# RWKV/HGRN2 decoder layer: the output projection's activations are loaded before the last column of a block and split behind it

## The chip, the cores and the metric

The kernel runs on one core of a Trainium2 chip. A core has five engines that run their own instruction lists in order and wait for each other by semaphores: TensorE (PE, with PEld for its weight loads), VectorE (DVE), ScalarE (ACT), GpSimd (POOL) and SyncE (SP). SP and POOL mainly issue transfers (DMAs) between the chip's memory (HBM) and the core's; PE's results go to PSUM banks. The metric is the device time of one execution in microseconds (us), the median of three runs.

## The reference

One decoder layer, 2048 tokens, model width 1024. Two kinds of head groups work beside each other on one input projection, their outputs go through one output projection, and a feed-forward part with a causal convolution follows.

```python
h = rmsnorm(x)
proj = h @ w_in                                    # 1024 -> 2048 (HGRN2) + 1792 (RWKV-7)
o_hg = hgrn2_mixer(*split(proj[:, :2048], 4))      # 4 heads of 128, chunked linear recurrence
o_rw = rwkv7_mixer(*split(token_shift(proj[:, 2048:])))   # 8 heads of 64: r, k, v, decay, a, gate
x = x + concat([o_hg, o_rw]) @ w_out               # the output projection, 1024 -> 1024
x = x + conv_ffn(rmsnorm(x), w_up, w_down)         # 1024 -> 2 x 2816 -> 1024
return rmsnorm(x)
```

All is float32. A product is made of three matmuls on parts of its factors: each factor is split into a high part (a cast, on ACT) and a low part (the rest, a subtraction on DVE), and high x high, high x low and low x high are summed.

## The kernel before

The program has two phases. Phase 1 (to about 1300 us) goes over the 2048 tokens in four blocks of 512. `dense()` issues its work as a list of jobs: for each block 30 columns ("P") of the input projection, each 128 wide, as eight k by three matmuls into one PSUM bank "pj"; and out blocks ("O"), the output projection of a block. Beside it, two other streams issue RWKV's work (per block two "supers" of 256 channels) and HGRN2's (per head of a block). A driver takes pieces of the streams in turn, and after that a scheduler in the framework sets each engine's order from the recorded program, so that instructions of the three streams stand mixed. Buffers come from pools by tag, each tag with a number of tiles; a tile that is still read makes the next writer wait.

The out block of block 0 (called Out 1 here, about 529 to 636 us) is issued after the last column of block 1, that of block 1 (Out 2, 883 to 971 us) after the last column of block 2, and that of block 2 (Out 3, 1209 to 1298 us) after the last column of block 3. Block 3's output projection belongs to phase 2 and is left as it is.

`out_block` (L379) works in four quarters: `i2` is the half of the tokens, `dh` the half of the 512-wide output columns. In each quarter two token tiles of 128 get one pj bank each, and for each of eight k the weights `woraw` are loaded by POOL (tag wraw, four tiles, L395), split into `wh` (ACT, L254) and `wl` (DVE, L255) in tag w (four tiles), and used by two times three matmuls with `hh` and `hl`. At the end the input `xh` is added to the banks (DVE, L413) and sent to `x1d`. I call three such matmuls a triple.

The activations come from `oT`, to which the mixers write. In Out 1 and Out 2 each k of the first quarter loads a row of 128 x 512 (`oraw`, SP, L388, tag sg, two tiles) and splits it into `hh` (ACT, L247) and `hl` (DVE, L248). Out 3 has the first half of its tokens ready in `ohl`, loaded and split during the last columns; at its third quarter it loads the second half in eight pieces of 128 x 256 (L392). In the quarter with such loads, `xh` takes two of the four wraw tiles; in the others it takes tag sg.

`load(i)` (L570) gets a column's weights, two tiles of tag w for high and low parts. From the second block on they come from HBM copies `Win`, with four DMAs on POOL. When a column starts, `load(i + 1)` gets those of the next one. For the last column of a block this is the first column of the block after the out block (`Win280`, `Win281`), so that its weights lie in two of the four w tiles while the out block runs.

Steps of the mixers that stand around the out blocks and are named later: `Ti` is built by DVE row by row (L811, L813), then transposed to `TZ` (L817) and `TTs` (L823); PE's small products with `M` and `RHS` follow, and then eight steps of the recurrence, `XH` (PE L915, L920, DVE L922). `KBT` and `E` of the next super are made by DMAs on SP from `KBb` (L766) and `Ed` (L757). `UV` is an ACT copy out of PSUM. In HGRN2, `SH` is the state, `part` and `osq` belong to the norm of its output, `hX`, `hk` and `hq` to its chunks. Tags s0, s1 and s2 hold RWKV's r, k, v of a super, tag tl its decay inputs.

## Time and profile before

| | |
|---|---|
| runs | 2632.3, 2635.08, 2636.21 us (median 2635.08) |
| profiled execution | 2639.41 us |
| its span | 2637.6 us |
| PE busy | 2545.3 us (97% of the span) |
| DVE busy | 1968.2 us (75%) |
| ACT busy | 1384.5 us (52%) |
| POOL busy | 381.7 us (14%) |

The profile is of one execution on the chip. A window gives busy times of each engine between two points of the span; "PEclk" is the clock that PE was granted, as a share of full speed. A timeline row gives the start, the duration, the engine, the line, the operation, what it writes and reads, how many instructions are merged in the row, and in brackets how long the engine had stood idle before it and which instruction ended that. A helper's line (L247, L248, L254, L255, L270 to L272) is shared by all that call it, so that the names of the tiles tell what is meant.

### The profile page before, as it was taken

Reading aid. Unit: us, or ns where it says so; the run is one execution under the profiler, and the core shown is the slowest. Engines: PE = TensorE matmul, PEld = TensorE weight load, DVE = VectorE, ACT = ScalarE, POOL = GpSimd, SP = SyncE. Lnnn points to the kernel's source line nnn. Section 1 sums busy time; section 2 is a strip of 40 time slices with the busy share of each in tenths; the row PEclk is TensorE's granted clock in tenths of the full one; section 3 lists DMA queues with packets and bytes.
Section 4 is the critical chain, followed back from the end, with each engine's and each line's share of the span. In section 5 each row is a group of like instructions: output and inputs, shape, how many; then the busy total and the mean of one; then the engine's idle time right before and its main releaser. Section 6 shows DMA issues by size and latency. Waiting matters only on the chain.

```text
span 2637.6 us, 51053 instructions
## 1 busy us (share of the span) xinstructions
PE 2545.3 (97%) x19467; PEld 2046.8 (78%) x19467; DVE 1968.2 (75%) x3744; ACT 1384.5 (52%) x2266; POOL 381.7 (14%) x686
## 2 busy tenths in 40 slices
PE   7999999989999899999899999999999999999998
PEld 6877777767777677777688888887888888888887
DVE  5878676775576765787678799987998887766556
ACT  5566454555446554355466754556554554545444
POOL 6433222212222122222100000000000000000000
PEclk9999999989999999999899999999999999999999
DMA  8846463545655566755574477746764554998655
GB/s 309 236 161 191 159 167 119 148 145 200 195 170 141 168 204 181 252 181 161 193 251 136 130 233 260 235 158 217 243 204 132 170 171 131 333 321 284 200 190 188
DMA packets 380298, 518.98 MB, mean 197 GB/s; under 512 B 114463, under 2 KB 211093, under 8 KB 380053
## 3 DMA queue, kind: packets, MB, share of 16 engines
q1 hardware_dynamic: 325521, 337.38, 40.3%
q0 software_dynamic: 54464, 178.32, 20.9%
q8 instruction: 153, 2.51, 0.4%
q14 instruction: 92, 0.75, 0.1%
q10 hardware_dynamic: 68, 0.02, 0.0%
HBM read 372.99 MB, written 134.22 MB: 192 GB/s over the span
## 4 chain that ended last, share of the span: by engine, by line
PE 53%; issue 7%; DVE 6%; DMA 5%; ACT 4%; POOL 1%; SPq 0%; DVEq 0%; POOLq 0%; ACTq 0%
PE ua L270 5%; PE ua L272 5%; PE ua L271 5%; PE pj L270 3%; PE da L271 3%; PE da L270 3%; PE da L272 3%; PE ud L271 3%; PE pj L271 3%; PE ud L270 3%; PE ud L272 3%; PE pj L272 3%; PE db L271 2%; PE db L272 2%; PE db L270 2%
## 5 line engine op out<-in xcount | busy, mean ns | idle before, releaser
L270 PE MATMUL pj<-hh,wh 128*128 128x512 f32 x960 | 394.6, 411 | 8.2 <-issue 3.4
L272 PE MATMUL pj<-hh,wl 128*128 128x512 f32 x960 | 378.3, 394 | 0.0
L271 PE MATMUL pj<-hl,wh 128*128 128x512 f32 x960 | 377.7, 394 | 0.0
L270 PE MATMUL ua<-Bh,uwh 128*128 128x512 f32 x704 | 276.6, 393 | 2.3 <-ACT m L122 1.2
L272 PE MATMUL ua<-Bh,uwl 128*128 128x512 f32 x704 | 274.9, 391 | 0.0
L271 PE MATMUL ua<-Bl,uwh 128*128 128x512 f32 x704 | 274.5, 390 | 0.0
L270 PEld LDWEIGHTS pj<-hh,wh 128*128 128x128 f32 x960 | 181.2, 189 | 56.6 <-issue 10.1
L272 PEld LDWEIGHTS pj<-hh,wl 128*128 128x128 f32 x960 | 180.8, 188 | 41.0 <-issue 2.0
L271 PEld LDWEIGHTS pj<-hl,wh 128*128 128x128 f32 x960 | 181.5, 189 | 34.6 <-issue 1.6
L254 ACT CAST uwh<-uraw 128x512 fp32r<-128x512 f32 x220 | 134.5, 617 | 131.2 <-PE ua L271 54.7
L255 DVE TENSOR_TENSOR dal<-draw,dah 128x512 fp32r<-128x512 f32 x138 | 95.3, 691 | 108.3 <-ACT dah L254 106.9
L255 DVE TENSOR_TENSOR uwl<-uraw,uwh 128x512 fp32r<-128x512 f32 x220 | 147.4, 686 | 34.1 <-ACT uwh L254 33.8
L254 ACT CAST dah<-draw 128x512 fp32r<-128x512 f32 x138 | 85.7, 621 | 160.8 <-PE da L271 75.9
L270 PEld LDWEIGHTS ua<-Bh,uwh 128*128 128x128 f32 x704 | 132.4, 188 | 32.0 <-ACT m L122 3.8
L272 PEld LDWEIGHTS ua<-Bh,uwl 128*128 128x128 f32 x704 | 132.4, 188 | 27.9 <-DVE uwl L255 0.4
L271 PEld LDWEIGHTS ua<-Bl,uwh 128*128 128x128 f32 x704 | 132.3, 188 | 26.9
L1506 POOL DMA_DIRECT2D gd<-y x2 | 1.1, 542 | 948.8 <-DVE y L1504 948.8
L270 PE MATMUL ud<-Bh,uwh 128*128 128x512 f32 x352 | 138.2, 393 | 0.0
L272 PE MATMUL ud<-Bh,uwl 128*128 128x512 f32 x352 | 137.3, 390 | 0.0
L271 PE MATMUL ud<-Bl,uwh 128*128 128x512 f32 x352 | 137.2, 390 | 0.0
L271 PE MATMUL da<-dbl,dah 128*128 128x512 f32 x332 | 129.6, 390 | 0.3 <-DVE dbl L255 0.3
L272 PE MATMUL da<-dbh,dal 128*128 128x512 f32 x332 | 129.4, 390 | 0.0
(582 smaller groups left out, 6226.7 us busy)
## 6 DMA issues: line engine op xcount, KB each, us to landing
uraw<-in_w_up_dram SPq DMA_DIRECT2D x176, 256.0 KB
woraw<-in_w_out_dram POOLq DMA_DIRECT2D x96, 256.0 KB, 3.5
br<-gd SPq DMA_DIRECT2D x88, 256.0 KB
draw<-Sg SPq DMA_DIRECT2D x88, 256.0 KB
draw<-Tw SPq DMA_DIRECT2D x88, 256.0 KB
gd<-y SPq DMA_DIRECT2D x86, 256.0 KB
Sg<-br SPq DMA_DIRECT2D x72, 256.0 KB
xt<-x1d SPq DMA_DIRECT2D x32, 512.0 KB
```

The lines of the kernel that those rows point to most:

```text
L254: S.copy(hi, src)
L255: V.tensor_sub(lo, src, hi.bitcast(F32))
L270: TE.matmul(acc, lh, rh, start=first, stop=False, skip_group_check=skip)
L271: TE.matmul(acc, lh, rl, start=False, stop=False, skip_group_check=skip)
L272: TE.matmul(acc, ll, rh, start=False, stop=last, skip_group_check=skip)
L1506: (dma if end is None else nc.gpsimd.dma_start)(gd_[2 * h + b][fb * P:(fb + 1) * P, :], ys[0][:, b * BLK:(b + 1) * BLK])
```

## The change

A job "L" is put before the last column of blocks 1, 2 and 3, which waits until the mixers have written the outputs of the block concerned. For Out 1 and Out 2 it runs `o_load`: three loads of two rows each into the tiles of tags s0, s1 and s2 (`opair`) and two loads of one row into tags tl and sg (`oraw`). Behind the last column's matmuls of each k, `next_out` splits the rows whose places in `hh` and `hl` that column has read. For Out 3 it runs `o_half`: two loads of four half rows (`ohalf`) into s0 and s1, which are split in the second quarter instead of the third. `xh` always takes tag sg. The next column's weights are not loaded when a last column starts; for Out 1 and Out 2 `ahead` loads them at k = 3 of the last quarter's second half, for Out 3, after which no column comes, there is nothing to load.

```diff
--- before.py
+++ after.py
@@ -376,28 +376,20 @@
                 ready[k] += 1
             return f
 
-        def out_block(nb, oh=None, ol=None, then=None):
+        def out_block(nb, oh=None, ol=None, then=None, ahead=None):
 
 
             for i2 in range(2):
                 for dh in range(2):
                     accs = [bank("pj") for _ in range(2)]
                     for k in range(KD):
-                        if i2 == 0 and dh == 0 and oh is None:
-                            raw = stg("sg", "oraw", 2)
-                            dma(raw, oT[nb][k * P:(k + 1) * P, :])
-                            split_to(hh[:, k, :], hl[:, k, :], raw)
-                        if i2 == 1 and dh == 0 and oh is not None:
-                            raw = stg("sg", "oraw", 2)[:, 0:256]
-                            dma(raw, oT[nb][k * P:(k + 1) * P, 256:512])
-                            split_to(hh[:, k, 256:512], hl[:, k, 256:512], raw)
+                        if i2 == 0 and dh == 1 and oh is not None:
+                            split_to(hh[:, k, 256:512], hl[:, k, 256:512], rows["O2"][k // 4][:, k % 4, :])
                         raw = wp.tile([P, 512], F32, tag="wraw", name="woraw", bufs=4)
                         wload(raw, w_out[0, k * P:(k + 1) * P, dh * 512:dh * 512 + 512])
                         wh, wl = split(wp, raw, [P, 512], "w", 4)
                         if k == KD - 2:
-                            inputs = dh == 0 and (i2 == 0) == (oh is None)
-                            xh = [wp.tile([P, BLK], F32, tag="wraw", name="xh", bufs=4) if inputs else
-                                  stg("sg", "xh", 2) for _ in range(2)]
+                            xh = [stg("sg", "xh", 2) for _ in range(2)]
                             for q in range(2):
                                 t0 = nb * BLK + (i2 * 2 + q) * P
                                 dma(xh[q], x[0, t0:t0 + P, dh * 512:dh * 512 + 512])
@@ -408,6 +400,8 @@
                             mm3(accs[q], lhs, (wh, wl), k == 0, k == KD - 1)
                             if i2 == 1 and dh == 1 and q == 1:
                                 next_block(then, k)
+                                if k == 3 and ahead is not None:
+                                    ahead()
                             yield 680
                     for q in range(2):
                         V.tensor_add(xh[q], accs[q], xh[q])
@@ -463,11 +457,41 @@
             act(h4, src, AF.Copy, scale=w)
             V.scalar_tensor_tensor(l4, src, w, h4.bitcast(F32), ALU.mult, ALU.subtract)
 
+        def behind(k):
+
+            return [k - 2] if 2 <= k < KD - 1 else [k - 2, k - 1, k] if k == KD - 1 else []
+
         def next_block(nb, k):
 
             if nb is not None and nb < NBLK:
-                for k_ in ([k - 2] if 2 <= k < KD - 1 else [k - 2, k - 1, k] if k == KD - 1 else []):
+                for k_ in behind(k):
                     split_h(nb, k_)
+
+        def o_load(nb):
+
+            pieces = []
+            for u in range(3):
+                t_ = sp.tile([P, 2, BLK], F32, tag=f"s{u}", name="opair")
+                dma(t_, oT[nb][2 * u * P:2 * (u + 1) * P, :].rearrange("(k p) t -> p k t", p=P))
+                pieces += [t_[:, 0], t_[:, 1]]
+            for tag, bufs in (("tl", 1), ("sg", 2)):
+                pieces.append(stg(tag, "oraw", bufs))
+                k = len(pieces)
+                dma(pieces[-1], oT[nb][(k - 1) * P:k * P, :])
+            rows[("P", nb)] = pieces
+
+        def o_half(nb):
+
+            rows["O2"] = []
+            for u in range(2):
+                t_ = sp.tile([P, 4, 256], F32, tag=f"s{u}", name="ohalf")
+                dma(t_, oT[nb][4 * u * P:4 * (u + 1) * P, 256:512].rearrange("(k p) t -> p k t", p=P))
+                rows["O2"].append(t_)
+
+        def next_out(nb, k):
+
+            for k_ in behind(k):
+                split_to(hh[:, k_, :], hl[:, k_, :], rows[("P", nb)][k_])
 
         def sum_load(m):
 
@@ -559,6 +583,8 @@
             for m in range(2):
                 extra += [(at[3] + 14 + 5 * m, ("E", sum_load(m))), (at[3] + 17 + 5 * m, ("E", sum_make(m)))]
             extra += [(at[3] + 25 + m, ("W", 2, o_take(m))) for m in range(4)]
+            extra += [(len(jobs) - 1, ("L", 2))]
+            extra += [(at[nb] - 2, ("L", nb - 2)) for nb in range(2, NBLK)]
             for i, jb in sorted(extra, key=lambda e: e[0], reverse=True):
                 jobs.insert(i, jb)
             cols = [jb[1] for jb in jobs if jb[0] == "P"]
@@ -605,9 +631,15 @@
                     if jb[0] == "W":
                         jb[2]()
                     else:
-                        yield from (out_block(2, *rows["O"]) if jb[1] == 2 else out_block(jb[1], then=jb[1] + 2))
+                        yield from (out_block(2, *rows["O"]) if jb[1] == 2 else out_block(jb[1], then=jb[1] + 2, ahead=lambda i=i: load(i)))
+                    continue
+                if jb[0] == "L":
+                    while done["rw1"] < 2 * jb[1] + 4 or done["rw2"] < 2 * jb[1] + 2 or done["hg"] < 4 * jb[1] + 4:
+                        yield None
+                    (o_half if jb[1] == 2 else o_load)(jb[1])
                     continue
                 _, col, ev, cond, fin = jb
+                after = jobs[n + 1][1] if jobs[n + 1][0] == "O" and jobs[n + 1][1] < 2 else None
                 while not cond():
                     yield None
                 load(i)
@@ -616,7 +648,8 @@
                     next(ahead)
                     next(ahead)
                     constants()
-                load(i + 1)
+                if jobs[n + 1][0] != "O":
+                    load(i + 1)
                 i += 1
                 acc = bank("pj")
                 then = jobs[n + 1][1] if jobs[n + 1][0] == "A" else None
@@ -632,6 +665,8 @@
                         if fin is not None:
                             fin()
                     next_block(then, k)
+                    if after is not None:
+                        next_out(after, k)
                     yield 648 + 436 * aside
 
         def last_dma(nb):
```

The order moves on all engines around the three out blocks and stays as it was elsewhere; each engine has as many instructions as before, but for the loads. Lines in the new program are 35 higher from `rw_super` on.

ACT in Out 1, from the part around HGRN2's norm on (`Sf`, `osq`, `VT`) with `UV` and `RHS` of RWKV. Before:

```order
L122 ACTIVATE Sf<-hf 128x256
L122 ACTIVATE osq<-hg,eps_71 128x512
L122 ACTIVATE osq<-osq 128x512
L122 ACTIVATE VT<-hg 128x512
L122 ACTIVATE UV<-rw 64x8x128 x2
L247 CAST hh<-oraw 128x512 x2
L122 ACTIVATE RHS<-rw 128x8x64
L122 ACTIVATE RHS<-rw 64x8x64 x2
L254 CAST wh<-woraw 128x512
L247 CAST hh<-oraw 128x512 x2
L254 CAST wh<-woraw 128x512 x3
L247 CAST hh<-oraw 128x512 x2
```

With the change, from the place where `KT` and `Af` are done:

```order
L254 CAST wh<-woraw 128x512
L247 CAST hh<-oraw 128x512
L254 CAST wh<-woraw 128x512
L122 ACTIVATE osq<-hg 128x512
L247 CAST part<-osq 128x512
L122 ACTIVATE Sf<-hf 128x256
L122 ACTIVATE sgm<-pj 128x512
L122 ACTIVATE UV<-rw 64x8x128 x2
L247 CAST hh<-opair 128x512 x2
L247 CAST hh<-oraw 128x512
L118 ACT_TABLE_LOAD
L122 ACTIVATE osq<-hg,eps_71 128x512
```

Five casts hh stand earlier, four of them ahead of the rows shown; `UV` stands behind `part`, `Sf` and `sgm`, and three casts hh behind it.

SP at the same place, which issues the transfers of RWKV's next super and then the out block's. Before:

```order
L949 DMA oT_144<-yo 128x2x512
L766 DMA KBT<-KBb 32x16x32 x3
L754 DMA Ed<-M 32x16x32 x4
L766 DMA KBT<-KBb 32x16x32 x2
L757 DMA E<-Ed 64x1024 x2
L766 DMA KBT<-KBb 32x16x32 x11
L388 DMA oraw<-oT_143 128x512 x2
```

With the change:

```order
L984 DMA oT_144<-yo 128x2x512
L480 DMA oraw<-oT_143 128x512
L475 DMA opair<-oT_143 128x2x512 x2
L801 DMA KBT<-KBb 32x16x32 x3
L789 DMA Ed<-M 32x16x32 x4
L801 DMA KBT<-KBb 32x16x32 x2
L792 DMA E<-Ed 64x1024 x2
L801 DMA KBT<-KBb 32x16x32 x11
L475 DMA opair<-oT_143 128x2x512
L480 DMA oraw<-oT_143 128x512
```

Three of the five loads moved ahead of the first `KBT` transfers of the super, two stand behind the last of them.

PE in Out 3, at the end of the second quarter, after the last triple with `ohl`. Before:

```order
L915 MATMUL rw<-XH,M 64x64 x4
L920 MATMUL rw<-AR,XH 64x64 x4
L1000 MATMUL hg<-hX 32x16 x13
L915 MATMUL rw<-XH,M 64x64 x4
L920 MATMUL rw<-AR,XH 64x64 x4
L1000 MATMUL hg<-hX 32x16 x3
L915 MATMUL rw<-XH,M 64x64 x4
L920 MATMUL rw<-AR,XH 64x64 x4
L1000 MATMUL hg<-hX 32x16 x16
L915 MATMUL rw<-XH,M 64x64 x4
L920 MATMUL rw<-AR,XH 64x64 x4
L1007 MATMUL hg<-hX 32x32 x8
```

With the change:

```order
L950 MATMUL rw<-XH,M 64x64 x4
L955 MATMUL rw<-AR,XH 64x64 x4
L270 MATMUL pj<-wh,hh 128x512
L271 MATMUL pj<-wl,hh 128x512
L272 MATMUL pj<-wh,hl 128x512
L270 MATMUL pj<-wh,hh 128x512
L271 MATMUL pj<-wl,hh 128x512
L272 MATMUL pj<-wh,hl 128x512
L270 MATMUL pj<-wh,hh 128x512
L271 MATMUL pj<-wl,hh 128x512
L272 MATMUL pj<-wh,hl 128x512
L950 MATMUL rw<-XH,M 64x64 x4
```

The steps of the recurrence (`XH`) stood next to each other or with small HGRN2 products between them; now three triples with `hh` and `hl` follow the step shown, and the next two as well.

## The prediction

> **What bounds the kernel now.** I read the page's first part, then cut the stretches around the three out blocks into windows, then looked at PE's idle times one by one, and last at what each releaser had itself been waiting for.

> ```profile
> span 2637.6 us, 51053 instructions
> PE 2545.3 (97%) x19467; PEld 2046.8 (78%) x19467; DVE 1968.2 (75%) x3744; ACT 1384.5 (52%) x2266; POOL 381.7 (14%) x686
> ```

> PE is busy for 97% of the span, so no other engine's saving counts unless it takes an idle moment of PE away or a stretch in which PE runs at a lower clock. The change touches only the out blocks and their surroundings. In the windows the columns are start:end and length, busy time (and instructions) of PE, PEld, DVE, ACT and POOL, then granted PE clock, DMA share, GB/s.

> ```profile
> 540.00:546.30 6.30, 1.82 (x11) 0.86 (x12) 5.91 (x22) 5.10 (x8) 0.00 (x0) 0.82 0.15 59
> 546.30:551.00 4.70, 4.70 (x131) 4.17 (x132) 4.70 (x17) 2.62 (x5) 0.00 (x0) 0.52 0.38 117
> 536.00:564.00 28.00, 19.03 (x292) 14.67 (x290) 25.23 (x82) 17.41 (x28) 2.54 (x5) 0.88 0.40 127
> 564.00:580.00 16.00, 14.84 (x183) 10.19 (x184) 12.10 (x26) 5.96 (x13) 3.14 (x7) 0.68 0.53 177
> 580.00:636.00 56.00, 54.32 (x644) 40.36 (x644) 34.63 (x67) 31.14 (x53) 10.96 (x21) 1.00 0.41 133
> 883.00:919.00 36.00, 29.95 (x413) 20.82 (x413) 28.27 (x68) 22.41 (x41) 5.59 (x10) 1.00 0.53 169
> 919.00:971.00 52.00, 49.93 (x639) 36.99 (x639) 39.91 (x82) 29.48 (x48) 10.30 (x20) 1.00 0.47 150
> 1248.00:1263.00 15.00, 8.84 (x335) 7.10 (x331) 9.87 (x30) 1.64 (x3) 0.67 (x2) 0.93 0.53 168
> 1263.00:1268.00 5.00, 4.94 (x12) 3.72 (x12) 3.50 (x7) 2.69 (x9) 0.00 (x0) 0.54 0.56 189
> ```

> This is where time can come from. Out 1 (block 0's out block): PE idle is 28.00 - 19.03 = 8.97 us and 1.16 us in its first part, 1.68 us later. At reduced clock it also loses 0.48 x 4.7 = 2.3 us behind 546.3 and 0.32 x 16 = 5.1 us behind 564. Out 2 (block 1's): 6.05 and 2.07 us idle, no clock lost. Out 3 (block 2's): 6.16 us idle in 1248 to 1263, then 0.46 x 5 = 2.3 us of clock. That is 26.1 us idle and 9.7 us of clock, so 36 us is a ceiling.

> Next, who ends the idle times: the number in brackets is the idle time ahead of the instruction and its releaser.

> ```profile
> 538.71 0.49 PE L1075 MATMUL hg<-hq,SH 128*128 128x128 f32 x2 [1.01 <-DVE SH L1067]
> 541.45 0.50 PE L1094 MATMUL hg<-part,ones 128*128 128x512 f32 x1 [1.34 <-ACT part L247]
> 546.26 0.54 PE L1000 MATMUL hg<-hq,hk 128*32 128x32 f32 x22 [2.14 <-DVE hk L957]
> 558.92 0.50 PE L270 MATMUL pj<-wh,hh 128*128 128x512 f32 x1 [1.52 <-ACT hh L247]
> 563.89 0.50 PE L270 MATMUL pj<-wh,hh 128*128 128x512 f32 x1 [1.96 <-ACT hh L247]
> 885.82 0.49 PE L1075 MATMUL hg<-hq,SH 128*128 128x128 f32 x2 [1.72 <-DVE SH L1067]
> 1259.48 0.39 PE L915 MATMUL rw<-XH,M 64*64 64x64 f32 x6 [1.03 <-DVE XH L922]
> 1263.06 0.79 PE L270 MATMUL pj<-wh,hh 128*128 128x512 f32 x1 [3.01 <-ACT hh L247]
> 1262.60 0.40 ACT L247 CAST hh<-oraw 128x256 fp32r<-128x256 f32 x1 [8.04 <-DMA oraw<-oT]
> PE pj L270: 8.6, 6
> DMA oraw<-oT: 10.9, 5
> ```

> The last two rows are of the view of tile oraw: PE waited 8.6 us in six goes for it or for what is split from it, and its engines stood 10.9 us for its DMA. So the load is the late thing: at 1262.60 the cast had waited 8.04 us for its DMA and PE 3.01 us for the cast. The other idle times of Out 1 are no matter of oraw: they end with SH, part and hk, on DVE, which in 536 to 564 is itself busy for 25.23 of 28 us. There DVE, not PE, is the bound; whatever still has to pass through it has to be paid.

> **The change part by part.** It does not drop any arithmetic. Splits, weight casts and matmuls of the out block are as many as before.

> Loads ahead, Out 1 and Out 2. Eight oraw loads become three loads of a pair (opair) and two single ones, issued before the last column.

> ```profile
> 520.50 8.63 SPq L766 DMA_DIRECT2D KBT<-KBb  x11
> 529.23 9.33 SPq L388 DMA_DIRECT2D oraw<-oT  x2
> L247 ACT CAST hh<-oraw x24: 393/613/623, 546.7 to 1277.6; 128x512 fp32r<-128x512 f32 x16, 128x256 fp32r<-128x256 f32 x8
> L248 DVE TENSOR_TENSOR hl<-oraw,hh x24: 418/684/693, 548.1 to 1278.0; 128x512 fp32r<-128x512 f32 x16, 128x256 fp32r<-128x256 f32 x8
> ```

> Before, SP issues them from 529.2, behind the eleven KBT transfers. Three of the five new loads stand ahead of all KBT transfers of that super, the other two where the old ones stood, so five of the eight rows of o are there before the out block needs them. The splits are 8 x 0.61 = 4.9 us on ACT and 8 x 0.68 = 5.5 us on DVE as before. They only stand earlier, among the Ti adds of RWKV. What goes in Out 1 are the two waits for hh, 1.52 + 1.96 = 3.5 us, and the idle time that the out block's triples, now ready, can fill.

> What comes in its place is in the new order: all eight k of the first quarter stand ahead of TZ, and TZ, TTs and the evictions xh close it.

> ```profile
> 544.65 2.05 ACT L122 ACTIVATE UV<-rw 64x1024 f32<-64x1024 f32 x2
> 564.48 1.06 DVE L817 STREAM_TRANSPOSE TZ<-Ti 128x512 f32<-128x512 f32 x1
> 566.14 2.89 DVE L823 STREAM_TRANSPOSE TTs<-TZ 32x512 f32<-32x512 f32 x4
> 535.94 0.62 ACT L254 CAST wh<-woraw 128x512 fp32r<-128x512 f32 x1 [1.66 <-PE pj L271]
> 561.27 0.69 DVE L255 TENSOR_TENSOR wl<-woraw,wh 128x512 fp32r<-128x512 f32 x1 [0.25 <-ACT wh L254]
> ```

> First, ACT's UV pair now stands behind part, Sf and sgm, and PE's UV,M products are early in the quarter: I price this wait at the pair and a cast's length on each side, 2.05 + 0.62 + 0.39 = 3.1 us. Second, the weights of k = 4 and 5 are split behind Ti adds: two casts and two subtractions, 2 x (0.62 + 0.69) = 2.6 us. Third, TZ and TTs take 1.06 + 2.89 = 3.95 us on DVE at the quarter's end, of which the remaining triples hide about half: 2.0 us. Behind the waiting TTs on DVE stand the two xh adds, which free the pj banks for the next quarter, and behind the waiting UV on ACT the last three hh casts. Together 7.7 us of new waits.

> Of the idle 10.1 us, the waits for SH, part and hk (1.01 + 1.34 + 2.14 = 4.5 us) are DVE's, and triples between them hide half, so 2.2 stay. Of the 7.4 us of clock I leave half, 3.7, since new waits near 2 us stay. Out 1's gain: 10.1 + 7.4 - 2.2 - 3.7 - 7.7 = 3.9 us. The ends: nothing comes off SH, part and hk and no clock returns, 10.1 - 4.5 - 7.7 = -2.1; or all the clock returns and half the new waits are hidden, 17.5 - 4.5 - 3.9 = 9.1.

> On the clock: the rows show 0.52 behind a stretch where PE was busy for 1.82 of 6.3 us with no gap over 2.14 us, and 0.68 behind a gap of 1.96. [...]

> Out 2 has the same edit. Its idle 6.05 us holds 1.72 us for SH and, in three goes, 2.1 us for hh (engine, line, waited for: total, times, longest):

> ```profile
> PE pj L270 <- ACT hh L247: 2.1, 3, 0.9
> ```

> Half of SH stays (0.9), the third wait (2.0) comes whole and the second with 2.0, as the weights here meet single Ti adds; UV stands where it stood, though RHS behind it now follows five hh casts. The gain is 6.05 - 0.9 - 2.0 - 2.0 = 1.2 us. The ends: only the hh waits go and 3.1 + 2.0 come, 2.1 - 5.1 = -3.0; or the waits for hh and SH go and nothing comes, 3.8.

> Out 3. Two loads of four rows (ohalf), ahead of the KBT transfers, replace eight loads at the third quarter. PE's order had five XH steps in a row without an out triple between them and then the wait of 3.01 us; now three triples follow each step, some 9 matmuls:

> ```profile
> 566.58 0.63 PE L271 MATMUL pj<-wl,hh 128*128 128x512 f32 x1
> 551.28 0.40 PE L271 MATMUL pj<-wl,hh 128*128 128x512 f32 x1
> ```

> The 0.63 is one at low clock, 0.40 one at full. So 6.16 us idle (the 3.01 and 3.15 between the steps) and 2.3 us of clock can go, 8.5 us. Given back: eight hl subtractions of half width now stand ahead of TZ on DVE, 8 x 0.418 = 3.3 us, and I let all of it through to PE since the M chain behind TTs is what PE needs. Gain 8.5 - 3.3 = 5.2 us. The ends: 3.0 - 3.3, about 0; 8.5.

> Four weight tiles, xh in sg. The next column's weights held two of the four w tiles for the whole out block.

> ```profile
> ACT wh L254 <- PE pj L272: 25.5, 16, 3.4
> 636.01 0.50 PE L270 MATMUL pj<-hh,wh 128*128 128x512 f32 x1 [0.61 <-DVE xh L413]
> 971.24 0.50 PE L270 MATMUL pj<-hh,wh 128*128 128x512 f32 x1 [0.64 <-DVE xh L413]
> ```

> ACT waits 25.5 us for a free tile, yet PE's idle time in 580 to 636 and 919 to 971 is 1.68 + 2.07 us, and 1.25 of it is the xh wait around the next column. I take 0.5 us, ends 0 and 2.5.

> Late weights of the next column. They are now loaded behind the out block's last woraw on POOL:

> ```profile
> 624.04 0.54 POOL L395 DMA_DIRECT2D woraw<-in_w_out_dram  x1 [3.07 <-DVE wl L255]
> 963.20 0.54 POOL L395 DMA_DIRECT2D woraw<-in_w_out_dram  x1 [5.04 <-DVE wl L255]
> wh<-Win280h POOLq DMA_DIRECT2D x3, 256.0 KB, 5.3
> ```

> With 5.3 us to land, the first is there at 624.6 + 5.3 = 629.9 of the 636.0 where the column starts; in Out 2 at 963.7 + 5.3 = 969.0 of 971.2, and the last of the four three issues (1.6 us) later, 970.6. Cover is 4 us and under 1. I take 0; without cover it is at most the landing, 5.3 each.

> Sum: 3.9 + 1.2 + 5.2 + 0.5 + 0 = 10.8 us. The profiled execution took 2639.41 us (span 2637.6), 4.3 above the median of the runs; it becomes 2628.6, and the median of 2635.08 becomes **2624** us.

> **The rivals.** A, no change, 28%: DVE is the bound around Out 1 and Out 2 (25.23 of 28), so idle time only moves from hh to wl, UV and TTs; or the last two of the five loads still land late. For it: the splits are no fewer. Against it: in 580 to 636 DVE has 21 us free. With Out 1 and 2 at the mean of 3.9 and -2.1 and of 1.2 and -3.0, that is 0 together, and Out 3 at half, 2.6 us: 2632.

> B, slower, 12%: the new gaps bring the low clock to Out 2. Place: the UV or TTs wait of the first quarter. Gaps of 1.96 and 2.14 us stood ahead of a low clock, 1.72 did not, so it decides from about 2 us, and I expect 2.0 and more there. Price: another 5.1 us as in 564 to 580. Out 1 -2.1, Out 2 -3.0 - 5.1, Out 3 +2.6: -7.6 us, 2643. Against it: Out 2 had full clock with 6 us idle.

> C, all comes back, 8%: all three at their upper ends and 1 us of tiles, 9.1 + 3.8 + 8.5 + 1.0 = 22.4 us: 2613. For it: filler triples beat short waits everywhere. Against it: UV's place in ACT's order.

> **How the numbers follow.** My forecast holds 52%; its own range is 2617 to 2630. The range reaches from C's 2613 over A to a little on the slower side, 2638, leaving about 2 in 10. What can be told from no change is 0.2%, 5.3 us. Faster: the forecast and C, 60%. Within: A, 29% with B's mild end. Slower: 11%.

> **What would show it.** Right: no PE wait on hh from opair or ohalf over 0.5 us; triples after each XH step in Out 3 and the clock at 1.00 there. The new waits should be UV (3.1 us), wl of k = 4 and 5, and the quarter's end on TTs. Wrong: a column behind Out 1 or Out 2 that waits for Win280 or Win281 by more than 1 us; an idle sum in Out 1 of over 10 us; a clock below 0.9 in Out 2. Phase 2, from 1300 us on, should not differ by more than 1 us.

## The result, and the profile after

The changed kernel takes 2618.28 us (median of 4 runs, 2616.32 to 2622.17), the kernel before 2635.64 us (median of 4, 2632.3 to 2639.75). The ratio is 0.9933, with a 95% interval of 0.9919 to 0.9946: 17.4 us faster, where 11 us were forecast. One execution of the last variant below took 3126.29 us at a granted clock of 0.75 and is left out of that variant's numbers.

The first part of the page of the changed kernel:

```profile
span 2620.3 us, 51021 instructions
PE 2540.9 (97%) x19467; PEld 2047.8 (78%) x19467; DVE 1962.9 (75%) x3744; ACT 1382.7 (53%) x2266; POOL 381.6 (15%) x686
```

PE still fills 97% of the span, so the page alone doesn't say where 17 us went. For that I cut both traces at the same points of the program: the end of the last column of a block (where an out block starts) and the first matmul of the next column (where it ends); for Out 3 the end is the first `wacc` product of the third kind in phase 2. The windows of the kernel before are the stretch ahead of Out 1, then Out 1, Out 2, Out 3, and phase 2 behind it; columns as in the prediction:

```profile
0.00:536.13 536.13, 508.53 (x5623) 401.08 (x5624) 386.79 (x919) 285.28 (x479) 186.95 (x325) 1.00 0.61 187
536.13:636.01 99.88, 88.06 (x1116) 65.08 (x1116) 71.84 (x174) 54.40 (x93) 16.63 (x31) 0.91 0.43 139
882.54:971.24 88.70, 80.34 (x1054) 58.28 (x1052) 68.85 (x151) 52.48 (x90) 16.13 (x30) 1.00 0.49 157
1209.01:1308.36 99.35, 84.33 (x1138) 64.88 (x1135) 68.72 (x163) 53.67 (x95) 17.07 (x31) 0.93 0.48 160
1308.36:2637.59 1329.23, 1314.41 (x5794) 1082.53 (x5794) 1053.93 (x1593) 705.83 (x1137) 13.99 (x26) 1.00 0.63 210
```

The same five of the changed kernel:

```profile
0.00:540.43 540.43, 512.79 (x5623) 404.13 (x5624) 386.82 (x916) 288.45 (x486) 184.22 (x321) 0.99 0.61 187
540.43:632.11 91.68, 83.47 (x1118) 63.84 (x1116) 71.70 (x177) 49.93 (x87) 18.78 (x35) 0.93 0.45 142
875.17:957.85 82.68, 76.48 (x1053) 59.80 (x1053) 66.34 (x155) 49.97 (x87) 17.53 (x33) 1.00 0.47 156
1193.83:1287.96 94.13, 83.98 (x1137) 63.68 (x1135) 66.06 (x163) 52.65 (x91) 16.87 (x31) 0.97 0.48 158
1287.96:2620.32 1332.36, 1315.65 (x5794) 1082.40 (x5794) 1053.54 (x1593) 705.78 (x1137) 13.99 (x26) 1.00 0.63 209
```

| stage | before | with the change | difference | forecast |
|---|---|---|---|---|
| Out 1 | 99.88 | 91.68 | -8.2 | -3.9 |
| Out 2 | 88.70 | 82.68 | -6.0 | -1.2 |
| Out 3 | 99.35 | 94.13 | -5.2 | -5.2 |
| ahead of Out 1 | 536.13 | 540.43 | +4.3 | 0 |
| phase 2 | 1329.23 | 1332.36 | +3.1 | 0 |

The out blocks gave 19.4 us. The columns between them (246.5 and 237.8 us before, 243.1 and 236.0 with the change) make -5.3 us, of which no run shows how much is the change's. What the change doesn't touch differs by some us from one profile to the next: over the profiles of all twelve kernels of this study the stretch ahead of Out 1 takes 535.0 to 540.4 us and phase 2 1327.5 to 1333.4 us. So below I read the stage that an edit touches, and the medians for the sum. Where two kernels have the same edit in a stage, the stages agree well in Out 1 and Out 2 (91.68 and 91.65, 82.68 and 82.28 us), and in Out 3 within some 3 us.

What PE waits for in Out 1, Out 2 and Out 3 of the changed kernel (engine, line, waited for: total, times, longest; a choice of the rows):

```profile
PE rw L878 <- ACT ZT L122: 2.8, 2, 2.6
PE pj L270 <- DVE hgg L370: 2.0, 1, 2.0
PE rw L826 <- ACT UV L122: 1.4, 1, 1.4
PE hg L1130 <- DVE part L248: 0.7, 1, 0.7
...
PE pj L271 <- DVE wl L255: 1.7, 2, 1.2
PE rw L865 <- DVE TZ L852: 1.1, 1, 1.1
...
PE pj L270 <- DVE xh L407: 1.0, 2, 0.7
```

The waits for hh, 8.6 us in six goes before, are gone from all three. SH and hk, 3.1 us of Out 1 before, are gone from it too. New in Out 1 are `hgg`, `UV` and a long `ZT`; new in Out 2 are `KT` (1.0 us) and `hk` (0.8).

### The profile page after: what moved, and what is told of

Read it like the earlier page. It is cut to its first block, busy times and chain, and to the rows that moved or that the text cites. A ratio compares the mean times of both kernels' runs of the same rounds, so it can differ in the third digit from the quotient of the medians.

```text
span 2620.3 us, 51021 instructions
## 1 busy us (share of the span) xinstructions
PE 2540.9 (97%) x19467; PEld 2047.8 (78%) x19467; DVE 1962.9 (75%) x3744; ACT 1382.7 (53%) x2266; POOL 381.6 (15%) x686
## 5 line engine op out<-in xcount | busy, mean ns | idle before, releaser
L270 PE MATMUL pj<-hh,wh 128*128 128x512 f32 x960 | 394.5, 411 | 3.8 <-ACT xt L122 1.6
L272 PE MATMUL pj<-hh,wl 128*128 128x512 f32 x960 | 378.7, 395 | 0.8 <-issue 0.6
L271 PE MATMUL pj<-hl,wh 128*128 128x512 f32 x960 | 378.3, 394 | 0.0
L270 PE MATMUL ua<-Bh,uwh 128*128 128x512 f32 x704 | 276.8, 393 | 3.6 <-ACT m L122 2.8
L272 PE MATMUL ua<-Bh,uwl 128*128 128x512 f32 x704 | 274.6, 390 | 0.0
L271 PE MATMUL ua<-Bl,uwh 128*128 128x512 f32 x704 | 274.4, 390 | 0.0
L270 PEld LDWEIGHTS pj<-hh,wh 128*128 128x128 f32 x960 | 181.3, 189 | 51.1 <-issue 6.4
L272 PEld LDWEIGHTS pj<-hh,wl 128*128 128x128 f32 x960 | 181.1, 189 | 41.1 <-issue 1.7
L271 PEld LDWEIGHTS pj<-hl,wh 128*128 128x128 f32 x960 | 181.6, 189 | 35.4 <-issue 2.2
L254 ACT CAST uwh<-uraw 128x512 fp32r<-128x512 f32 x220 | 134.4, 617 | 130.3 <-PE ua L271 56.1
L255 DVE TENSOR_TENSOR dal<-draw,dah 128x512 fp32r<-128x512 f32 x138 | 95.2, 690 | 113.1 <-ACT dah L254 111.5
L255 DVE TENSOR_TENSOR uwl<-uraw,uwh 128x512 fp32r<-128x512 f32 x220 | 147.2, 685 | 35.1 <-ACT uwh L254 35.0
L254 ACT CAST dah<-draw 128x512 fp32r<-128x512 f32 x138 | 85.8, 622 | 165.1 <-PE da L271 76.7
L270 PEld LDWEIGHTS ua<-Bh,uwh 128*128 128x128 f32 x704 | 132.3, 188 | 34.0 <-ACT m L122 6.4
L272 PEld LDWEIGHTS ua<-Bh,uwl 128*128 128x128 f32 x704 | 132.2, 188 | 28.0 <-DVE uwl L255 0.4
L271 PEld LDWEIGHTS ua<-Bl,uwh 128*128 128x128 f32 x704 | 132.3, 188 | 26.6
L270 PE MATMUL ud<-Bh,uwh 128*128 128x512 f32 x352 | 138.2, 392 | 0.0
L272 PE MATMUL ud<-Bh,uwl 128*128 128x512 f32 x352 | 137.3, 390 | 0.0
L271 PE MATMUL ud<-Bl,uwh 128*128 128x512 f32 x352 | 137.2, 390 | 0.0
L271 PE MATMUL da<-dbl,dah 128*128 128x512 f32 x332 | 129.6, 390 | 0.3 <-DVE dbl L255 0.2
L272 PE MATMUL da<-dbh,dal 128*128 128x512 f32 x332 | 129.4, 390 | 0.0
## 6 DMA issues: line engine op xcount, KB each, us to landing
uraw<-in_w_up_dram SPq DMA_DIRECT2D x176, 256.0 KB
woraw<-in_w_out_dram POOLq DMA_DIRECT2D x96, 256.0 KB, 3.8
br<-gd SPq DMA_DIRECT2D x88, 256.0 KB
draw<-Sg SPq DMA_DIRECT2D x88, 256.0 KB
draw<-Tw SPq DMA_DIRECT2D x88, 256.0 KB
gd<-y SPq DMA_DIRECT2D x86, 256.0 KB
Sg<-br SPq DMA_DIRECT2D x72, 256.0 KB
```

What stands on the lines that cost most here:

```text
L254: S.copy(hi, src)
L255: V.tensor_sub(lo, src, hi.bitcast(F32))
L270: TE.matmul(acc, lh, rh, start=first, stop=False, skip_group_check=skip)
L271: TE.matmul(acc, lh, rl, start=False, stop=False, skip_group_check=skip)
L272: TE.matmul(acc, ll, rh, start=False, stop=last, skip_group_check=skip)
```

## The experiments

All kernels below compute the whole output. Each line of a diff is against the kernel named ahead of it.

### Two weight tiles again

The changed kernel, with the next column's weights loaded when the last column starts:

```diff
-                if jobs[n + 1][0] != "O":
-                    load(i + 1)
+                load(i + 1)
```

> The change, but the next column's weights are again loaded when the last column starts and hold two of the four w tiles through Out 1 and Out 2. Theory A (the early loads and the earlier splits make the gain; the tiles are worth 0.5 us as in the prediction): 2619 us, Out 1 and Out 2 within 1 us of the change's 91.7 and 82.7 us. Rival B (the triples of the out block stall in short moments for their weights, which the idle times do not show; PE's busy time in Out 2 fell by 3.9 us with the change at an unchanged clock): Out 1 and Out 2 each 2 to 4 us longer, 2623 to 2626 us.

Measured: 2619.94 us (2617.24 to 2622.71), ratio to before 0.9942 (0.9928 to 0.9956). Out 1 takes 91.23 us and Out 2 84.42 us. Theory A's time holds: 1.3 us from the tiles, all of it in Out 2, which is 1.7 us longer where theory A allowed 1. Rival B was right about the kind of the loss and wrong about its size. The time that PE spends on the tile pj in Out 2 (start:end, length, then PE, PEld, DVE, ACT) before, with the change, and with two tiles:

```profile
882.54:971.24 88.70, 53.75 (x194) 33.52 (x193) 5.38 (x8) 0.59 (x1) 1.00 0.49 157
...
875.17:957.85 82.68, 51.26 (x193) 34.50 (x193) 5.34 (x8) 0.59 (x1) 1.00 0.47 156
...
872.52:956.94 84.42, 52.74 (x193) 33.81 (x192) 5.36 (x8) 0.59 (x1) 1.00 0.45 146
```

The same 192 matmuls of the out block count as 53.75 us busy before and 51.26 with the change, at full clock in all three (the counts of 193 and 194 take in matmuls at the edges). With the change, three rows of 0.39 us that follow each other from 887.15 us on start 0.23 us apart, while the matmul at 882.88 us, which had waited 0.53 us, is shown with 0.51 us and the next one starts 0.34 us behind it: part of what a stop costs counts as busy time. Two tiles bring back 1.5 of those 2.5 us.

### The splits inside the first quarter

The changed kernel, whose rows are still loaded ahead, but split where they were split before:

```diff
+                        if i2 == 0 and dh == 0 and oh is None and k < KD - 1:
+                            for k_ in ([k] if k < KD - 2 else [k, k + 1]):
+                                split_to(hh[:, k_, :], hl[:, k_, :], rows[("P", nb)][k_])
...
-                    if after is not None:
-                        next_out(after, k)
```

> The change, but the eight rows of Out 1 and Out 2, though loaded ahead as in the change, are split inside the first quarter, each at its k as before (row 7 with row 6). Theory A1 (the late DMA was the cause: PE waited 8.6 us for hh, and ACT's cast had waited 10.9 us for oraw): most of the gain stays, Out 1 at most 93 us and Out 2 at most 84 us, about 2620 us. Rival A2 (the place of the splits was the cause, since DVE is busy for 25 of 28 us there): Out 1 97 us or more and Out 2 87 us or more, about 2629 us.

Measured: 2610.83 us (2608.49 to 2613.08), ratio 0.991 (0.9894 to 0.9925), below the change's interval. Out 1 and Out 2:

```profile
536.41:623.84 87.43, 80.91 (x1117) 61.35 (x1115) 71.01 (x177) 49.84 (x87) 18.33 (x35) 0.96 0.45 149
868.09:949.82 81.73, 77.17 (x1053) 60.20 (x1052) 66.14 (x155) 50.27 (x87) 17.39 (x33) 1.00 0.47 158
```

A1 holds, and more than holds: with the splits back in the first quarter the whole gain stays, and splitting behind the last column is no gain at all but costs 4.2 us in Out 1. The scheduler places the first splits nearly alike in both; what differs is the end of the first quarter, where one xh addition now stands ahead of TTs on DVE and triples stand between the TZ products on PE. PE's wait of 2.6 us for ZT isn't there.

### The early loads alone

The variant above, with the next column's weights and Out 3 as in the kernel before: early loads for Out 1 and Out 2 are what is left of the change, and with them the place of `xh`, which stays in tag sg in their first quarter, where the kernel before puts it in two of the four wraw tiles.

```diff
...
-            extra += [(len(jobs) - 1, ("L", 2))]
...
-                if jobs[n + 1][0] != "O":
-                    load(i + 1)
+                load(i + 1)
```

> The kernel before with the early loads alone: the eight rows of Out 1 and Out 2 are loaded ahead of the last column and split inside the first quarter; Out 3 and the next column's weights are as before. Theory A1 (the late DMA was the cause, and the rest is small): Out 1 88 to 90 us, Out 2 82 to 84 us, Out 3 98 to 99 us, about 2616 us. Rival W (the early loads need the four w tiles, which alone took 5.9 us off Out 1): Out 1 92 us or more, 2621 us or more.

Measured: 2626.41 us (2624.49 to 2628.38), ratio 0.9966 (0.9953 to 0.9978). The stages:

```profile
539.11:630.79 91.68, 83.33 (x1117) 61.58 (x1116) 72.60 (x178) 51.21 (x88) 16.65 (x31) 0.94 0.41 133
874.16:957.98 83.82, 79.13 (x1054) 59.41 (x1053) 66.59 (x153) 51.05 (x88) 16.00 (x30) 1.00 0.45 144
```

The early loads with this place of `xh` take 8.2 us off Out 1 and 4.9 off Out 2. What the two wraw tiles that `xh` leaves free are worth was not tested by itself. ACT's wait for the weights' DMA, where they would show first, is 0 in Out 1 of both kernels, and 3.3 us before and 2.5 here in Out 2. The time as a whole fell by 8.7 us only; the stretch ahead of Out 1 (539.1 us) and phase 2 (1333.4) of this profile are among the longest seen, and why isn't shown. Of the two expectations, Out 2 has theory A1's length, but the time is rival W's (2621 us or more), and Out 1 at 91.7 is nearer to it. With the splits inside, the tiles do matter in Out 1 (87.43 against 91.68), other than with the splits behind the column (91.68 against 91.23). In Out 2 of this pair the tile pj is busy for 53.40 us with two w tiles and 51.24 with four, much as in the pair above.

### The weight tiles alone

The kernel before, with the next column's weights loaded at k = 3 of the last quarter:

```diff
+                                if k == 3 and ahead is not None:
+                                    ahead()
...
-                load(i + 1)
+                if jobs[n + 1][0] != "O":
+                    load(i + 1)
```

> The kernel before with one part of the change: the next column's weights are loaded at k = 3 of the last quarter instead of when the last column starts, so that Out 1 and Out 2 have four w tiles. Theory A: 2635 us, Out 1 99.4 and Out 2 88.2 us (0.5 us off the two together). Rival B: Out 1 and Out 2 each 2 to 4 us shorter, 2628 to 2632 us.

Measured: 2631.66 us (2627.74 to 2640.24), ratio 0.9992 (0.9979 to 1.0005), not to be told from no change. But the stages moved: Out 1 from 99.88 to 93.95 us and Out 2 from 88.70 to 91.76. Neither theory had that, though the median lies where rival B put it. In the first part of Out 2 there are two spells at half clock; here the piece ahead of the first, the two spells, and PE's longest wait:

```profile
887.58:891.00 3.42, 2.83 (x62) 1.79 (x62) 2.86 (x6) 2.42 (x6) 0.49 (x1) 1.00 0.27 77
891.00:897.83 6.83, 6.83 (x34) 3.85 (x34) 5.34 (x12) 3.40 (x8) 1.12 (x3) 0.50 0.65 200
914.89:918.30 3.41, 3.41 (x30) 2.71 (x20) 1.96 (x3) 0.62 (x1) 0.44 (x1) 0.50 0.35 108
...
914.04 0.69 PE L894 MATMUL rw<-M 64*64 64x64 f32 x32 [3.34 <-DVE AR L900]
```

PE ran 10.2 us at half clock, 5.1 us lost, where the kernel before had full clock. Only the last 3.41 of them follow the new wait of 3.34 us for `AR`, as rival B of the prediction would have it. The other 6.83 us came before that wait, behind a piece in which PE was busy for 2.83 of 3.42 us; no long wait stands there.

### Out 3 as before

The changed kernel without `o_half`; Out 3 loads and splits in its third quarter and xh of that quarter lies in wraw:

```diff
-                        if i2 == 0 and dh == 1 and oh is not None:
-                            split_to(hh[:, k, 256:512], hl[:, k, 256:512], rows["O2"][k // 4][:, k % 4, :])
+                        if i2 == 1 and dh == 0 and oh is not None:
+                            raw = stg("sg", "oraw", 2)[:, 0:256]
+                            dma(raw, oT[nb][k * P:(k + 1) * P, 256:512])
+                            split_to(hh[:, k, 256:512], hl[:, k, 256:512], raw)
...
```

> The change for Out 1 and Out 2 alone; Out 3 loads and splits its second half in its third quarter as before. Theory A (Out 3's own edit made its stage 5.2 us shorter): Out 3 back at about 99.4 us from 94.1, 2623.5 us. Rival C (Out 3 became shorter because what precedes it arrives in another state, or by chance): Out 3 stays under 96 us, 2619 us.

Measured: 2621.98 us (2619.75 to 2623.58), ratio 0.9949 (0.9935 to 0.9963), 3.7 us above the change. Out 3:

```profile
1190.69:1289.14 98.45, 84.15 (x1137) 64.97 (x1135) 68.48 (x163) 53.72 (x95) 17.08 (x31) 0.94 0.50 162
```

98.45 us against 94.13, 4.3 us. Over all profiles, the four kernels with Out 3 as before take 97.3 to 99.4 us there (mean 98.3), and the eight with its edit 92.2 to 95.2 (mean 93.4): 4.9 us, theory A's size. Rival C's size falls, since Out 3 does not stay under 96 us. But what precedes Out 3 does move it: of the eight, the four kernels with the splits behind the last column take 94.0 to 95.2 us and the four with the splits inside the first quarter 92.2 to 92.6, though none of the edits between them touches Out 3's own code.

### The subtraction done twice

The changed kernel, with DVE's part of each split of Out 1 and Out 2 repeated:

```diff
                 split_to(hh[:, k_, :], hl[:, k_, :], rows[("P", nb)][k_])
+                V.tensor_sub(hl[:, k_, :], rows[("P", nb)][k_], hh[:, k_, :].bitcast(F32))
```

> The change, but behind each split of Out 1 and Out 2 the subtraction that makes hl is done a second time on DVE (the same values; 8 x 0.68 = 5.5 us more DVE work in each of the two out blocks, and PE has to wait for the second one). Theory D (rival A of the prediction: around the first quarter DVE is the bound, so whatever passes through it is paid): Out 1 and Out 2 each 4 to 5.5 us longer than the change's 91.7 and 82.7 us, about 2628 us. Rival (DVE's work there hides behind triples that are ready): each under 2 us longer, 2618 to 2621 us.

Measured: 2623.63 us (2621.99 to 2625.84), ratio 0.9958 (0.9945 to 0.9972). Out 1 93.00 us (+1.3), Out 2:

```profile
874.63:960.98 86.35, 77.93 (x1054) 59.51 (x1053) 70.70 (x163) 50.48 (x87) 17.54 (x33) 0.98 0.46 149
...
885.00 0.49 PE L1111 MATMUL hg<-hq,SH 128*128 128x128 f32 x2 [3.17 <-DVE SH L1103]
...
882.46:885.88 3.42, 0.88 (x7) 0.89 (x8) 3.42 (x13) 0.00 (x0) 0.00 (x0) 1.00 0.04 8
885.88:889.29 3.41, 2.92 (x10) 2.24 (x9) 3.37 (x12) 1.22 (x2) 1.08 (x2) 0.50 0.32 118
```

that is +3.7. Of 11 us put on DVE, 5.0 came through to the stages and 5.3 to the median, about half. DVE is neither the bound that rival A made it nor free. Part of Out 2's 3.7 us is clock: PE waits 3.17 us for `SH`, which now stands behind the doubled subtractions on DVE, and the next 3.41 us run at half clock.

### More room for the weights' loads

In the changed kernel the wait for ZT has a chain of its own. POOL, ACT and PE in the order of time:

```profile
559.35 0.54 POOL L389 DMA_DIRECT2D woraw<-in_w_out_dram  x1 [13.05 <-DVE Ti L848]
562.30 0.62 ACT L254 CAST wh<-woraw 128x512 fp32r<-128x512 f32 x1 [2.90 <-DMA woraw<-in_w_out_dram]
566.88 1.31 ACT L254 CAST wh<-woraw 128x512 fp32r<-128x512 f32 x2 [0.90 <-DMA woraw<-in_w_out_dram]
568.21 1.56 ACT L122 ACTIVATE ZT<-rw 32x256 f32<-32x256 f32 x4
568.64 0.31 PE L878 MATMUL rw<-TTs,ZT 32*32 32x32 f32 x2 [2.59 <-ACT ZT L122]
```

As I read it, POOL stands 13 us until a wraw tile is free (its split waits on DVE behind the Ti adds), so that weights are loaded late, ACT waits for them twice, and ZT stands behind those casts. POOL's stand alone is not new: it is 15.2 us at this place in the kernel before, and 16.5 us in the variant with the splits inside, where ACT waits 3.7 and 1.5 us for the weights while PE has triples to do. The edit gives half of these loads the tiles s0 to s2, which are empty by then:

```diff
+                        if oh is None and i2 == 0 and k % 4 >= 2:
+                            if k % 2 == 0:
+                                pair = sp.tile([P, 2, BLK], F32, tag=f"s{(2 * dh + k // 4) % 3}", name="wopair")
+                            raw = pair[:, k % 2]
+                        else:
+                            raw = wp.tile([P, 512], F32, tag="wraw", name="woraw", bufs=4)
```

> The change, but in the first two quarters of Out 1 and Out 2 the weights woraw of k = 2, 3, 6 and 7 are loaded into the tiles of tags s0, s1 and s2 (wopair) instead of wraw, so that loads need not wait for a wraw tile; nothing else is edited. Theory G (after the change the weights' loads are the next late thing: POOL waited 13 us for a wraw tile whose split stands behind DVE's Ti adds, ACT waited 2.9 and 0.9 us for woraw, and behind those casts stood ZT, for which PE waited 2.6 us): ACT's wait for the weights' DMA under 1 us, PE's wait for ZT under 0.5 us, Out 1 at 88 to 89 us from 91.7, 2615 us. Rival H (the quarter's end itself, TZ, TTs and the xh adds behind TTs, sets it): Out 1 91 us or more, 2618 us.

Measured: 2612.92 us (2606.88 to 2618.32), ratio 0.991 (0.9893 to 0.9927).

```profile
535.01:624.23 89.22, 81.46 (x1116) 61.87 (x1115) 71.70 (x177) 50.70 (x87) 17.67 (x33) 0.96 0.46 146
866.82:947.80 80.98, 76.37 (x1053) 59.18 (x1053) 66.31 (x155) 50.27 (x87) 16.20 (x31) 1.00 0.48 157
...
563.07 0.28 PE L883 MATMUL rw<-TTs,ZT 32*32 32x32 f32 x9 [1.05 <-issue]
```

Theory G holds in the main: PE's wait for ZT is gone, and of the 2.59 us before the TTs,ZT products 1.05 are left, for which the profile shows no releaser. Out 1 is 2.5 us shorter and Out 2 1.7. ACT still waits 1.9 us for the weights' DMA, more than expected, but no longer for 2.9 us at once, and 1.7 us of waits for wl are new on PE. The two intervals, of this kernel and of the change, just overlap.

The same edit on the variant with the splits inside:

> The same edit to the variant with the splits inside the first quarter (2610.8 us; Out 1 87.4, Out 2 81.7 us), in which PE's wait for ZT was already gone. Theory G: no more than 1 us from Out 1 and Out 2 each, 2609 to 2611 us. Rival H: no difference in either. A third case (the loads that run ahead crowd others): Out 1 or Out 2 2 us longer, 2613 us.

Measured: 2611.96 us (2608.37 to 2613.84), ratio 0.9905 (0.9891 to 0.9919); Out 1 87.53 us, Out 2 81.60, as without it. In that variant the wait was gone already, so that the edit finds nothing to take away.

### Another last column

The variant with the splits inside, with HGRN2's v as the last column of each block instead of g, for PE's wait of 2.0 us on hgg:

```diff
-                        for i, ev in enumerate((ev_q, ev_f, ev_v, ev_g)):
+                        evs = list(enumerate((ev_q, ev_f, ev_v, ev_g)))
+                        for i, ev in (evs if j < 3 else evs[:2] + [evs[3], evs[2]]):
...
```

> The variant with the splits inside the first quarter (2610.8 us, Out 1 87.4 us), and the last column of a block is now HGRN2's v instead of its gate g, so that its pj bank is freed by one ACT copy rather than by DVE's hgg, for which PE's second bank waited 1.9 us in Out 1. Theory E (that wait goes and nothing else moves): Out 1 85.5 us, Out 2 and Out 3 0 to 0.6 us shorter, 2608 us. Rival F (freed triples run ahead, so that fewer are left to cover TZ, TTs and the recurrence): Out 1 89 us or more, 2613 us or more.

Measured: 2611.06 us (2605.22 to 2613.4), ratio 0.9905 (0.9891 to 0.9919). Out 1:

```profile
538.05:622.01 83.96, 78.97 (x1117) 59.79 (x1115) 69.04 (x177) 50.12 (x87) 18.47 (x35) 1.00 0.47 152
```

The wait for hgg is gone, and the stage is 3.5 us shorter, with no half clock at all; Out 2 is 1.5 us longer, 83.23. Theory E's wait came out in Out 1. The median can't tell its 2608 us from the 2610.83 without this edit.

With v last in block 1 alone, and the room for the weights:

```diff
+                        evs, swap = list(enumerate((ev_q, ev_f, ev_v, ev_g))), nb == 1 and j == 3
+                        for i, ev in (evs[:2] + [evs[3], evs[2]] if swap else evs):
...
```

> The variant of the line above, and the last column of block 1 alone is HGRN2's v instead of g (that gave Out 1 84.0 us, with PE's clock at full there, and cost 1.5 us in Out 2 where block 2's last column was changed too). Theory E: Out 1 84 us, Out 2 81.5 us, 2607 us. Rival F (Out 1's gain was the phase of the clock's low spells in one execution): Out 1 87 us, 2610 us.

Measured: 2608.7 us (2606.97 to 2612.62), ratio 0.9899 (0.9884 to 0.9914), the lowest median of the study. The stages:

```profile
536.32:621.13 84.81, 80.82 (x1117) 61.10 (x1116) 69.28 (x177) 50.49 (x88) 17.46 (x33) 0.98 0.47 151
865.54:946.38 80.84, 77.27 (x1053) 60.18 (x1052) 66.12 (x155) 50.52 (x87) 16.31 (x31) 1.00 0.48 158
```

Theory E's stages came out, and rival F's 87 us did not; that the whole beats the variant with the splits inside (2610.83 us) can't be told, their intervals overlap.

## Why the prediction was right, and where its sizes were off

**What bounds.** "So the load is the late thing" was right: the early loads, with nothing else of the change but the place of `xh`, took 8.2 and 4.9 us off Out 1 and Out 2, and the waits for hh are gone. These waits were 3.5 and 2.1 us, so more than their length came off, and the rest is order, clock and short stops.

**The ceiling.** The step that failed is the one that took idle time and lost clock as all there was to win. In Out 2 idle time fell from 88.70 - 80.34 = 8.4 to 6.2 us, 2.2 us, not far from the 1.2 of the forecast. The other 3.9 us of its 6.0 came out of PE's busy time, at a clock of 1.00 in both. 2.5 of them are the triples' (tile pj), which, as I read it, stopped less often: 36 of its rows last 0.47 us or more before and 25 with the change. The run with two weight tiles gives 1.5 of those to the tiles. Where the other 1.4 us went isn't shown. So PE's busy share is no measure here of how much there is to win: the same matmuls of the out block took 53.75 us of busy time before and 51.26 with the change. I read the page's 97% as if it left 3%.

**Out 1, 3.9 forecast, 8.2 measured.** Of the sum's terms: SH, part and hk were to keep half of 4.5 us, and kept 0.7. (The prediction put all three to DVE; its own row has part ended by a cast on ACT.) UV, priced at 3.1 (3.3 with two full casts of 0.62), took 1.4. The weights of k = 4 and 5 were to cost 2.6, and PE shows 0.4 us for wh in the whole stage and none for wl. TZ and TTs, priced at 2.0, took 2.8, of which 1.0 stood there before. Not in the sum were 2.0 us for hgg: the out block's second bank is the last column's, and its eviction stands on DVE among the Ti adds. So 9.9 us of waits were priced and about 7 came. On the clock 3.7 us were to be won; by the stage's mean, 0.09 x 99.88 - 0.07 x 91.68 = 2.6 were, give or take 1 us, since the clock is given to 0.01. About 2 us that are left are again busy time.

**What is late next** was named only in part. TZ and TTs at the quarter's end were right as the place, but what stood there was ZT behind two weight casts whose DMA was late, for want of a wraw tile. The prediction counted w tiles and not wraw tiles.

**Out 2, 1.2 forecast, 6.0 measured.** SH was to keep 0.9 us and kept nothing. The new wait for wl, priced at 2.0, did not come: the 1.7 us of the changed kernel stood there before as well. TZ has 1.1 us instead of 0.5, where 2.0 were priced as new. `KT` and `hk`, 1.8 us, were not in the sum. The rest is the ceiling's fault above. The rows of the kernel before, of Out 1 and of Out 2:

```profile
PE rw L843 <- ACT ZT L122: 1.0, 2, 0.5
...
PE pj L271 <- DVE wl L255: 1.7, 3, 1.2
PE rw L830 <- DVE TZ L817: 0.5, 1, 0.5
```

**Out 3, 5.2 and 5.2.** The means over all profiles say 4.9. The wait for hh and those on XH are gone, and the clock is 1.00 up to the boundary of the phases:

```profile
1193.83:1281.81 87.98, 81.90 (x1133) 62.52 (x1130) 64.90 (x161) 50.72 (x88) 15.93 (x30) 1.00 0.46 147
```

That 3.3 us were given back, as priced, isn't shown: no wait for TTs or M over 0.2 us stands there. What the rows show is idle time down from 15.0 to 10.2 us, 4.9 of the 6.16 counted on, and busy time down by 0.35 only, where 2.3 us of clock were to come back. So the sum was right with a term in it that was not seen, and its agreement to a tenth is luck.

**Four tiles**, 0.5 us: 1.3 in the stages, 1.7 in the medians. **Late weights of the next column**, 0: PE waited for none of them; their loads went out at 614 and 942 us, 18 and 15 us ahead of the columns, since POOL is done with woraw earlier than the rows of before said.

**The rivals.** A's 2632 us is far off; its reason (DVE is the bound) is half right, since half of the doubled subtraction comes through. B did not happen in the change. Its mechanism, a long wait and then the low clock in Out 2, did with the doubled subtraction (3.17 us for SH), and in part with the weight tiles alone. B's limit of about 2 us for a wait does not hold: gaps of 1.34 and 1.56 us, too, stood ahead of half clock, as the last section shows. C's 2613 is what the variants with the splits inside reach, not the change. That phase 2 would not differ by more than 1 us was too tight: it differs by up to 6 us between profiles, with the same code in that phase. As a whole the 17.4 us lie in the forecast's own range, 2617 to 2630, at its fast end: the place and the cause were right, and Out 1 and Out 2 were sized at 5.1 us together where 14.2 came.

## What to carry to other kernels

Load early and convert late: the early DMA brought most of the gain, and moving the conversion ahead as well cost 4 us in Out 1, where the order at the end of the first quarter came out worse. When a wait is removed, follow every tile tag that the same work uses (here wraw, w and pj) to see whose release comes last, because the next stall stood there in this case (PE's 2.6 us for ZT, behind weights for which POOL had waited 13 us until a wraw tile was free). Cut both traces at the same points of the program, since stages tell differences of 2 us which medians of whole runs can't; and check with a second kernel that has the same edit, because one profile of a stage can be off by as much.

## What was not expected of the hardware

```profile
540.58:543.99 3.41, 1.54 (x6) 0.80 (x6) 3.06 (x12) 2.48 (x5) 0.00 (x0) 1.00 0.12 45
543.99:550.82 6.83, 4.69 (x133) 4.06 (x132) 6.78 (x22) 4.63 (x8) 0.00 (x0) 0.50 0.24 70
...
138.34:141.75 3.41, 1.84 (x69) 1.29 (x68) 3.38 (x9) 1.99 (x3) 2.00 (x4) 1.00 0.72 203
141.75:151.99 10.24, 10.24 (x138) 7.00 (x137) 8.72 (x22) 9.22 (x22) 1.31 (x3) 0.50 0.36 140
...
1810.33:1813.74 3.41, 1.02 (x4) 0.86 (x5) 3.41 (x4) 1.67 (x3) 0.00 (x0) 1.00 0.42 145
1813.74:1817.15 3.41, 3.41 (x9) 2.63 (x8) 3.41 (x7) 1.14 (x2) 0.00 (x0) 0.50 0.45 161
...
1812.72 0.50 PE L271 MATMUL fa<-uwl,uwh 128*128 128x512 f32 x1 [2.76 <-DVE uwl L255]
```

PE was busy for 1.54, 1.84 and 1.02 of the 3.41 us ahead, and the longest single gaps were 1.34, 1.56 and 2.76 us, two of them under the 2 us from which the prediction's rival B saw a low clock. The spells last 3.41, 6.83 or 10.24 us in both profiles, but for the last of each, which goes on past the end of the span: one, two or three pieces. In one execution the pieces keep their beat: the spells at 543.99 and 1813.74 us, before, start 1269.75 us apart, 372 times 3.413, and the others of that profile stand on the same beat to 0.01 us. Where the beat lies differs between executions: counted in such pieces from the start of the span, at 1.27 us before (543.99) and at 1.80 with the change (551.35), so the same stop may or may not fall into one piece. At the same place of phase 2 the variant with the splits inside had a gap of 1.80 us, was busy for 1.79 us of the 3.42 shown around it, and kept its clock:

```profile
1780.60:1784.02 3.42, 1.79 (x8) 1.49 (x9) 2.83 (x5) 1.58 (x2) 0.00 (x0) 1.00 0.25 83
1784.02:1787.43 3.41, 3.18 (x14) 2.30 (x13) 3.41 (x6) 1.14 (x2) 0.00 (x0) 1.00 0.57 182
```
